# Block 1 of a two-block layer kernel: chunk decays inside the first chain, two output tiles among the attention, residual on VectorE, later gates

## The chip, the cores and the metric

The kernel runs on one core of a Trainium2 chip. The metric is device microseconds of one execution, as the median of several runs. The core has five engines that run beside each other and wait for one another on semaphores: TensorE (PE, matrix products into PSUM; its weight loads are listed apart as PEld), VectorE (DVE), ScalarE (ACT), GpSimd (POOL) and SyncE (SP), which only issues DMAs here. PSUM is the accumulator memory, SBUF the working memory.

## The reference, cut to what matters

512 tokens of width 1024 pass through two residual blocks, all in float32.

```python
# first_block
proj  = rms_norm(x, norm_pre_w) @ w_in            # 32 column tiles of 128, and 8 columns for beta and decay
beta  = sigmoid(d_b);  g = -exp(a_log) * softplus(d_a + dt_bias)
gc    = cumsum(g)                                  # per chunk: the "decays" exp(gc), exp(gc_last - gc)
o     = gated_delta_rule(silu(conv(d_q)), silu(conv(d_k)), silu(conv(d_v)), g, beta)   # 4 heads ("gdn")
mixed = concat([moba_attention(a_q, a_k, a_v) * silu(a_z), rms_norm(o) * silu(d_z)]) @ w_out
x     = x + rms_norm(mixed, norm_post_w)           # the residual
# second_block, token mixers: 8 channel groups i of 7 projections each
p  = rms_norm(x, norm1_g) @ w_in                   # 56 tiles: xa, ga, vb, bb, cb, ma, mb for every i
ya = rg_lru(conv(xa), gates r and i from two 128x128 matrices) * gelu(ga)
yb = bb * conv(cb * vb);  x = x + (sigmoid(ma)*ya + sigmoid(mb)*yb) @ w_out
# then a PEER layer: top-16 of product keys, 16384 experts, and a last norm
```

## The kernel before, in words

Activations lie transposed, channels on the 128 partitions and 512 tokens along the free axis. Every projection is kept near float32 by a split: an operand becomes a high part `hi` (in the format fp32r, by ScalarE, L194 or L258) and a low part `lo` (the difference, on VectorE or GpSimd, L195 or L259), and `mm3` adds three products, hi·hi, lo·hi and hi·lo. One output tile of 128 channels by 512 tokens is thus 8 slices of the contraction times 3, which makes 24 matmuls (L219). `wblock` loads one 128-column block of a weight matrix (512 KB), casts the high part on ScalarE and subtracts on GpSimd unless told otherwise; three such blocks fit (`WB = 3`). The tag `mm` of the pool `pmm` has two PSUM banks, the tags `pg` and `pt` two each, and `pu` of the pool `ps2` two.

The order of PE's instructions in blocks 1 and 2 is the program's own (`manual_schedule`). The order on the other engines comes from a planner at build time, which puts the instructions in a list by its own estimates; each engine then works through its list in order, and an instruction that waits holds up what stands behind it.

Block 1 begins with the norm statistics while the tiles 0 and 1 of the projection run slice by slice (L640), and computes beta and the decay logarithms `gl_` from 8 extra columns (L643 to L656). The generator `filler` yields after every matmul of the remaining 30 projection tiles; `pump(n)` takes n of them. `pump(54)` comes first. Then two small matmuls sum `gl_` into `gc` (L660, L661) and four small instructions make `gc`, `ngc`, `egc`, `egl`. After that a loop runs up to two gated-delta chains (`gdn(h)`) and one attention chain (`attn(j)`) at a time; after each step of a chain it pumps some filler (6 matmuls divided by the chains that run). The last steps of `gdn` normalize a head (`on`, L531), let three loop turns pass, and transpose it into `mixed` (L535). `attn` ends with `oa` (L591), a transpose (L595) and a copy into `mixed` (L596).

When all chains are done, the eight slices of `mixed` are multiplied with the silu gates `zg` (L695) and split into the `xhi` and `xlo` buffers, which the projection's operands held until then. The output projection follows, eight tiles of 24 matmuls (L704), with squares (L274) for the second norm. Its factor `rb2` is a power on GpSimd (L292), transposes (L295) and a ScalarE copy (L296). 16 small matmuls (`warm`, L183) run behind it. The residual (L721, L722) multiplies `mo` by `rb2` and adds the input `xk`; five slices are on VectorE, the slices 2, 5 and 7 (`XPOOL`) on GpSimd. As slices come out they are split (L258, L259), squared for block 2's first norm, and multiplied into block 2's first three tiles at once (L738), which `g.ahead` holds.

Block 2 loops over the channel groups i. For i = 0 the three tiles xa, ga, vb come from `g.ahead`; xa is scaled (L798), convolved (L809, L811) and split to `xch` and `xcl`; then come the gate products `pr` and `pi` (L822), and behind them in PE's order the tiles bb, cb, ma and mb, and for i = 1 again xa.

## Time and profile before

| | us |
|---|---|
| median of 3 runs (2138.79 to 2141.41) | 2138.96 |
| the profiled execution | 2143.05 |
| its span on the chip | 2141.3 |
| TensorE busy in the span | 2059.9 |
| VectorE busy | 1553.5 |
| GpSimd busy | 1000.3 |
| ScalarE busy | 845.9 |

All stretches are given in microseconds from the start of the span. Block 1 takes the first 423 or so, the residual and the start of block 2 reach to about 500, block 2 runs to roughly 750, and the PEER layer takes the rest. A row of the timeline that ends in x8 stands for eight instructions, and its second number is the stretch they cover. The number in brackets is the time for which the engine sat idle before, and who released it. The granted clock of TensorE is a share of full speed: 1.00 is 2.4 GHz, 0.50 is 1.2 GHz. A matmul of 512 columns counts as busy for its whole passage, so PE can be fully busy at half the clock.

### The profile page before, as it was taken

Reading aid. Unit: us, or ns where it says so; the run is one execution under the profiler, and the core shown is the slowest. Engines: PE = TensorE matmul, PEld = TensorE weight load, DVE = VectorE, ACT = ScalarE, POOL = GpSimd, SP = SyncE. Lnnn points to the kernel's source line nnn. Section 1 sums busy time; section 2 is a strip of 40 time slices with the busy share of each in tenths; the row PEclk is TensorE's granted clock in tenths of the full one; section 3 lists DMA queues with packets and bytes.
Section 4 is the critical chain, followed back from the end, with each engine's and each line's share of the span. In section 5 each row is a group of like instructions: output and inputs, shape, how many; then the busy total and the mean of one; then the engine's idle time right before and its main releaser. Section 6 shows DMA issues by size and latency. Waiting matters only on the chain.

```text
span 2141.3 us, 28911 instructions
## 1 busy us (share of the span) xinstructions
PE 2059.9 (96%) x10584; PEld 1783.5 (83%) x10584; DVE 1553.5 (73%) x2663; ACT 845.9 (40%) x1340; POOL 1000.3 (47%) x834
## 2 busy tenths in 40 slices
PE   8999999979999999887999999999999999999998
PEld 5787887758887878776999999999999999999886
DVE  5535446276777776999996897878787888887674
ACT  4434434344444444233454333333333333333333
POOL 3544252445566554775784254444444444444220
PEclk8999999979999999999999999999999999999999
DMA  4101121212322323222458999889889888898573
GB/s 154 54 30 50 55 70 54 79 60 89 98 89 89 99 89 109 83 76 69 183 230 302 319 353 313 301 301 310 297 307 309 293 311 302 300 313 271 192 257 101
DMA packets 147149, 394.07 MB, mean 184 GB/s; under 512 B 11584, under 2 KB 60864, under 8 KB 145216
## 3 DMA queue, kind: packets, MB, share of 16 engines
q1 hardware_dynamic: 110144, 258.00, 35.6%
q0 software_dynamic: 36864, 134.23, 18.1%
q8 instruction: 83, 1.36, 0.3%
q14 instruction: 58, 0.48, 0.1%
HBM read 364.92 MB, written 27.26 MB: 183 GB/s over the span
## 4 chain that ended last, share of the span: by engine, by line
PE 51%; DVE 8%; POOL 1%; DMA 1%; issue 1%; ACT 0%; POOLq 0%; DVEq 0%; SPq 0%; ACTq 0%
PE acc L1181 24%; PE ups L219 22%; PE gp L1074 4%; DVE t L1035 1%; DVE idxf L1006 1%; POOL pr L1002 1%; DVE ind L1037 1%; DVE ind L1034 1%; DVE eq L998 1%; DVE val L1036 1%; DMA gate<-gd 1%; DVE val L1033 1%; DVE cand L977 0%; DVE wlo L195 0%; DVE pos L1037 0%
## 5 line engine op out<-in xcount | busy, mean ns | idle before, releaser
L194 ACT CAST whi<-wraw 128x1024 fp32r<-128x1024 f32 x248 | 260.1, 1049 | 420.4 <-PE ups L219 290.8
L195 POOL TENSOR_TENSOR wlo<-wraw,whi 128x1024 fp32r<-128x1024 f32 x127 | 312.7, 2468 | 225.4 <-ACT whi L194 222.6
L1102 POOL DMA_INDIRECT row<-u,idx x128 | 199.1, 1556 | 267.8 <-DVE row L1108 228.3
L1102 POOL DMA_INDIRECT row<-v,idx x128 | 182.4, 1425 | 279.3 <-DVE xtok L1120 267.8
L219 PE MATMUL mm<-xhi,whi 128*128 128x512 f32 x856 | 234.7, 406 | 5.2 <-ACT xhi L194 3.6
L1181 PE MATMUL acc<-vhi,cl 128*128 128x512 f32 x768 | 237.6, 390 | 0.0
L1181 PE MATMUL acc<-vlo,ch 128*128 128x512 f32 x768 | 237.1, 389 | 0.4 <-DVE vlo L195 0.4
L1181 PE MATMUL acc<-vhi,ch 128*128 128x512 f32 x768 | 237.0, 389 | 0.0
L219 PE MATMUL mm<-xhi,wlo 128*128 128x512 f32 x856 | 233.2, 403 | 0.0
L219 PE MATMUL mm<-xlo,whi 128*128 128x512 f32 x856 | 226.9, 397 | 0.0
L219 PE MATMUL ups<-xhi,whi 128*128 128x384 f32 x1024 | 206.4, 339 | 7.9 <-DVE best L1033 6.6
L219 PE MATMUL ups<-xlo,whi 128*128 128x384 f32 x1024 | 202.9, 337 | 0.0
L219 PE MATMUL ups<-xhi,wlo 128*128 128x384 f32 x1024 | 201.9, 336 | 0.0
L219 PEld LDWEIGHTS ups<-xhi,whi 128*128 128x128 f32 x1024 | 182.1, 189 | 17.8 <-issue 8.7
L219 PEld LDWEIGHTS mm<-xhi,whi 128*128 128x128 f32 x856 | 157.6, 192 | 40.6 <-issue 8.0
L219 PEld LDWEIGHTS mm<-xhi,wlo 128*128 128x128 f32 x856 | 159.4, 191 | 36.8 <-issue 5.1
L219 PEld LDWEIGHTS mm<-xlo,whi 128*128 128x128 f32 x856 | 156.9, 189 | 34.3 <-issue 4.9
L195 DVE TENSOR_TENSOR wlo<-wraw,whi 128x1024 fp32r<-128x1024 f32 x121 | 149.1, 1232 | 49.7 <-ACT whi L194 49.7
L219 PEld LDWEIGHTS ups<-xlo,whi 128*128 128x128 f32 x1024 | 180.0, 189 | 0.1
L219 PEld LDWEIGHTS ups<-xhi,wlo 128*128 128x128 f32 x1024 | 179.8, 188 | 0.0
L194 ACT CAST ch<-act 128x384 fp32r<-128x384 f32 x128 | 65.7, 513 | 269.6 <-PE acc L1181 269.2
L1181 PEld LDWEIGHTS acc<-vlo,ch 128*128 128x128 f32 x768 | 144.1, 188 | 30.9 <-DVE vlo L195 0.8
(462 smaller groups left out, 3535.4 us busy)
## 6 DMA issues: line engine op xcount, KB each, us to landing
wraw<-uT SPq DMA_DIRECT2D x128, 512.0 KB
vring<-v SPq DMA_DIRECT2D x128, 512.0 KB
wraw<-w SPq DMA_DIRECT2D x88, 512.0 KB
gd<-stage SPq DMA_DIRECT2D x12, 2048.0 KB
gate<-gd SPq DMA_DIRECT2D x32, 768.0 KB
wraw<-wo SPq DMA_DIRECT2D x16, 512.0 KB
wraw<-wq SPq DMA_DIRECT2D x16, 512.0 KB
xr<-xT SPq DMA_DIRECT2D x8, 256.0 KB
```

The source lines that it names most:

```text
L194: nc.scalar.copy(hi, src)
L195: return (lo_eng or nc.vector).tensor_tensor(out=lo, in0=src, in1=hi.bitcast(F32), op=OP.subtract)
L219: nc.tensor.matmul(out, w(k), x(k), start=j == 0, stop=j == len(ps) - 1)
L998: V.tensor_tensor(out=eq[:, :n], in0=rank[:, :n], in1=pf[:, q].rearrange("p t k -> p (t k)")[:, None, :].to_broadcast([128, n, 16]), op=OP ...
L1002: nc.gpsimd.tensor_tensor(out=pr[:, :n].rearrange("p c (t k) -> p c t k", t=4), in0=eq[:, :n].rearrange("p c (t k) -> p c t k", t=4), in1= ...
L1006: V.tensor_reduce(out=g.idxf[:, :, h * 16 + 4 * q:h * 16 + 4 * q + 4], in_=pr[:, :n].rearrange("p c (t k) -> p t k c", t=4), axis=AX.X, op ...
L1033: V.max(out=v[:, 0:8], in_=x)
L1034: V.max_index(out=i[:, 0:8], in_max=v[:, 0:8], in_values=x)
L1035: V.match_replace(out=y[:, :n], in_to_replace=v[:, 0:8], in_values=x, imm_value=-3.0e38)
L1074: nc.tensor.matmul(ps[:, j * 128:(j + 1) * 128], oh[:, 1, j, :], oh[:, 0, j, :], start=True, stop=True)
L1102: nc.gpsimd.indirect_dma_start(out=r, out_offset=None, in_=g.a[tab], in_offset=bass.IndirectOffsetOnAxis(ap=s.idx[:, i:i + 1], axis=0))
L1181: nc.tensor.matmul(acc[m][e], l[:, ts], r[:, e * 512:(e + 1) * 512], start=False, stop=end and l is cl)
```

## The change

- The low part of the weight block of tile 1 is subtracted by VectorE, no longer by GpSimd.
- The two `gcp` matmuls and the five instructions behind them move into the first chain, behind two more of its turns (`decays`), and no longer stand ahead of the loop.
- `filler` goes on after the projection: for each slice k of `mixed`, once it is there, it does the gate product and the split (`merge`) and the slice's three products for the output tiles 0 and 1 (`first_out`). Slice 3, the last head pair of the attention, follows after the loop. The tiles 2 to 7 run as before.
- The transposes that end a `gdn` chain come six turns after its normalization, not three.
- All eight slices of the residual are on VectorE, in order. The warm-up matmuls there are 8, not 16. Squares are added in pairs (`add_pair`) and sent to the statistics in five sets of four products, not two. The last products are cut so that the power on GpSimd lies beside six of them.
- In block 2, i = 0, the tiles bb and cb are multiplied ahead of the gate products, into the two banks of `pu`.

```diff
@@ -137,10 +137,9 @@
 
 WB = 3
 WARM = 16
-WARM2 = 16
+WARM2 = 8
 PRE = 54
 VLO = (3, 4)
-XPOOL = (2, 5, 7)
 
 
 class K:
...
@@ -273,6 +273,18 @@
             self.sq = self.pool.tile([128, T], F32, name="ssq", tag="cth")
         self.g.nc.scalar.activation(self.sq, src, AF.Square)
 
+    def add_pair(self):
+
+        k, self.n = self.n, self.n + 1
+        if k < KD - 2 and k % 2 == 0:
+            self.acc = self.sq
+            return
+        if k < KD - 2:
+            self.g.nc.vector.tensor_tensor(out=self.sq, in0=self.acc, in1=self.sq, op=OP.add)
+        for tt in range(4):
+            self.g.nc.tensor.matmul(self.st[:, tt:tt + 1], self.sq[:, tt * 128:(tt + 1) * 128], self.g.ones,
+                                    start=k == 1 and tt == 0, stop=k == KD - 1 and tt == 3)
+
     def add(self):
 
         k, self.n = self.n, self.n + 1
@@ -285,11 +297,19 @@
 
     def finish(self, rb, rtok, tag="pg", dim=1024, eps=1e-6):
 
+        self.root(rtok, dim, eps)
+        self.spread(rb, rtok, tag)
+
+    def root(self, rtok, dim=1024, eps=1e-6):
         g = self.g
         nc = g.nc
         ms = self.pool.tile([128, 4], F32, name="ms")
         nc.vector.tensor_scalar(out=ms, in0=self.st[:, :4], scalar1=1.0 / dim, scalar2=eps, op0=OP.mult, op1=OP.add)
         nc.gpsimd.tensor_tensor(out=rtok, in0=ms, in1=g.nhalf[:, :4], op=OP.pow)
+
+    def spread(self, rb, rtok, tag="pg"):
+        g = self.g
+        nc = g.nc
         bc = g.pg.tile([128, 512], F32, name="bc", tag=tag)
         for tt in range(4):
             nc.tensor.transpose(bc[:, tt * 128:(tt + 1) * 128], rtok[:, tt:tt + 1].to_broadcast([128, 128]), g.ident)
@@ -399,6 +419,28 @@
             for i, k in enumerate((4, 5, 6, 7, 0, 1, 2, 3)):
                 yield from gate_in(24 + i, k)
 
+            o1["hi"], o1["lo"], o1["rb"], o1["rtok"] = operands(g)
+            o1["w"] = [wblock(g, g.a["wo1"][k]) for k in range(2)]
+            o1["ps"] = [g.pmm.tile([128, 512], F32, name="mm", tag="mm") for k in range(2)]
+            for k in (4, 5, 6, 7, 0, 1, 2):
+                while ("m", k) not in done:
+                    yield "blocked"
+                merge(k)
+                yield from first_out(k)
+
+        o1 = {}
+
+        def merge(k):
+            V.tensor_tensor(out=mixed[:, k, :], in0=mixed[:, k, :], in1=zg[:, k, :], op=OP.mult)
+            split(g, o1["hi"][:, k, :], o1["lo"][:, k, :], mixed[:, k, :])
+
+        def first_out(k):
+
+            for (h_, l_), ps in zip(o1["w"], o1["ps"]):
+                for j, (w, x) in enumerate(((h_, o1["hi"]), (l_, o1["hi"]), (h_, o1["lo"]))):
+                    nc.tensor.matmul(ps, w[:, k, :], x[:, k, :], start=k == 4 and j == 0, stop=k == 3 and j == 2)
+                    yield
+
 
         def gdn(h):
             dk, dq, dv = [res.pop((n, h)) for n in ("dk", "dq", "dv")]
@@ -421,9 +463,14 @@
             fq = R.tile([128, 4], F32, name="fq")
             V.tensor_tensor(out=fv, in0=rk, in1=beta[:, :, h], op=OP.mult)
             V.tensor_tensor(out=fa, in0=fv, in1=rk, op=OP.mult)
-            V.tensor_tensor(out=fk, in0=fa, in1=egc[:, :, h], op=OP.mult)
             V.tensor_scalar(out=fq, in0=rq, scalar1=128.0 ** -0.5, scalar2=None, op0=OP.mult)
             yield
+            if h == 0:
+
+                yield
+                yield
+                decays()
+            V.tensor_tensor(out=fk, in0=fa, in1=egc[:, :, h], op=OP.mult)
 
             gb = four(lambda o, b: nc.tensor.transpose(o, gc[:, b, h:h + 1].to_broadcast([128, 128]), g.ident))
             E = t4("E", "cth")
@@ -529,11 +576,11 @@
             V.tensor_tensor(out=ro, in0=ro, in1=fq, op=OP.mult)
             on = t4("on", bufs=2)
             V.tensor_tensor(out=on, in0=po, in1=ro[:, :, None].to_broadcast([128, 4, 128]), op=OP.mult)
-            yield
-            yield
-            yield
+            for _ in range(6):
+                yield
             ps = four(lambda o, b: nc.tensor.transpose(o, on[:, b, :], g.ident))
             nc.scalar.activation(mixed[:, 4 + h, :].rearrange("p (b t) -> p b t", b=4), ps, AF.Copy, scale=vec(g, "gnw", 0))
+            done.add(("m", 4 + h))
 
 
         def attn(j):
@@ -594,6 +641,7 @@
             yield
             ps = four(lambda o, b: nc.tensor.transpose(o, oa[:, b, :], g.ident), "pt")
             nc.scalar.copy(mixed[:, j, :].rearrange("p (b t) -> p b t", b=4), ps)
+            done.add(("m", j))
 
         warm(g, WARM)
         gate = P.tile([128, 8], F32, name="gate")
@@ -623,7 +671,7 @@
 
         with tc.manual_schedule(engines={mybir.EngineType.PE}):
 
-            w0 = [wblock(g, None, raw=g.w0[i], lo_eng=(V, nc.gpsimd)[i]) for i in range(2)]
+            w0 = [wblock(g, None, raw=g.w0[i], lo_eng=V) for i in range(2)]
             p0 = [g.pmm.tile([128, 512], F32, name="mm", tag="mm") for i in range(2)]
             st = RmsSum(g, R)
             pba = g.pg.tile([128, 512], F32, name="bap", tag="pt")
@@ -655,19 +703,22 @@
             softplus(g, P, fl(gl_), fl(z), 16)
             V.tensor_tensor(out=gl_, in0=gl_, in1=nea[:, None, :].to_broadcast([128, 4, 4]), op=OP.mult)
             pump(PRE)
-
-            ps = g.pg.tile([128, 512], F32, name="gcp", tag="pg")
-            nc.tensor.matmul(ps[:, :16], g.cst[:, C_U:C_U + 128], fl(gl_), start=True, stop=True)
-            nc.tensor.matmul(ps[:, 16:32], g.ones.to_broadcast([128, 128]), fl(gl_), start=True, stop=True)
             gc = P.tile([128, 4, 4], F32, name="gc")
             ngc = P.tile([128, 4, 4], F32, name="ngc")
             egc = P.tile([128, 4, 4], F32, name="egc")
             egl = P.tile([128, 4, 4], F32, name="egl")
-            V.tensor_copy(fl(gc), ps[:, :16])
-            V.tensor_scalar(out=fl(ngc), in0=ps[:, :16], scalar1=-1.0, scalar2=None, op0=OP.mult)
-            nc.scalar.activation(egc, gc, AF.Exp)
-            V.tensor_tensor(out=fl(egl), in0=ps[:, 16:32], in1=fl(gc), op=OP.subtract)
-            nc.scalar.activation(egl, egl, AF.Exp)
+
+            def decays():
+
+                ps = g.pg.tile([128, 512], F32, name="gcp", tag="pg")
+                nc.tensor.matmul(ps[:, :16], g.cst[:, C_U:C_U + 128], fl(gl_), start=True, stop=True)
+                nc.tensor.matmul(ps[:, 16:32], g.ones.to_broadcast([128, 128]), fl(gl_), start=True, stop=True)
+                V.tensor_copy(fl(gc), ps[:, :16])
+                V.tensor_scalar(out=fl(ngc), in0=ps[:, :16], scalar1=-1.0, scalar2=None, op0=OP.mult)
+                nc.scalar.activation(egc, gc, AF.Exp)
+                V.tensor_tensor(out=fl(egl), in0=ps[:, 16:32], in1=fl(gc), op=OP.subtract)
+                nc.scalar.activation(egl, egl, AF.Exp)
+
             mixed = g.xp.tile([128, 8, T], F32, name="mixed", tag="xr")
             zg = P.tile([128, 8, T], F32, name="zg")
             ready = {}
@@ -690,10 +741,10 @@
                     pump(-(-FILL // max(len(run), 1)))
                 if not run:
                     pump(FILL)
-            mhi, mlo, rb2, rt2 = operands(g)
-            for k in (4, 5, 6, 7, 0, 1, 2, 3):
-                V.tensor_tensor(out=mixed[:, k, :], in0=mixed[:, k, :], in1=zg[:, k, :], op=OP.mult)
-                split(g, mhi[:, k, :], mlo[:, k, :], mixed[:, k, :])
+            merge(3)
+            for _ in first_out(3):
+                pass
+            mhi, mlo, rb2, rt2 = o1["hi"], o1["lo"], o1["rb"], o1["rtok"]
 
             xk = [R.tile([128, T], F32, name=f"xk{k}", tag=("dk", "dq", "dv", "qT")[k % 4]) for k in range(KD)]
             for k in range(KD):
@@ -701,7 +752,7 @@
             mo = g.xp.tile([128, 8, T], F32, name="mo", tag="xr")
             st = RmsSum(g, R)
             for k in range(KD):
-                ps = proj_tile(g, wblock(g, g.a["wo1"][k]), mhi, mlo, (4, 5, 6, 7, 0, 1, 2, 3))
+                ps = o1["ps"][k] if k < 2 else proj_tile(g, wblock(g, g.a["wo1"][k]), mhi, mlo, (4, 5, 6, 7, 0, 1, 2, 3))
                 if k:
                     st.add()
                 st.square(ps)
@@ -717,26 +768,26 @@
             st = RmsSum(g, R)
 
             def residual(k):
-                e = nc.gpsimd if k in XPOOL else V
-                e.tensor_tensor(out=mo[:, k, :], in0=mo[:, k, :], in1=rb2, op=OP.mult)
-                e.tensor_tensor(out=mo[:, k, :], in0=mo[:, k, :], in1=xk[k], op=OP.add)
-
-            for k in XPOOL + (0, 1):
+                V.tensor_tensor(out=mo[:, k, :], in0=mo[:, k, :], in1=rb2, op=OP.mult)
+                V.tensor_tensor(out=mo[:, k, :], in0=mo[:, k, :], in1=xk[k], op=OP.add)
+
+            def products(k, tiles=(0, 1, 2)):
+                for t in tiles:
+                    (h_, l_), o = w[t], g.ahead[t]
+                    for j, (wt, x) in enumerate(((h_, g.b2[0]), (l_, g.b2[0]), (h_, g.b2[1]))):
+                        nc.tensor.matmul(o, wt[:, k, :], x[:, k, :], start=k == 0 and j == 0, stop=k == KD - 1 and j == 2)
+
+            for k in range(KD):
                 residual(k)
-            for k in range(KD + 1):
-                if k + 2 < KD and k + 2 not in XPOOL:
-                    residual(k + 2)
-                if k < KD:
-                    scaled_split(g, g.b2[0], g.b2[1], mo, "n1", [k])
-                    st.square(mo[:, k, :])
-                    st.add()
-                else:
-                    st.finish(g.b2[2], g.b2[3])
+                scaled_split(g, g.b2[0], g.b2[1], mo, "n1", [k])
+                st.square(mo[:, k, :])
                 if k:
-                    for o, (h_, l_) in zip(g.ahead, w):
-                        for j, (wt, x) in enumerate(((h_, g.b2[0]), (l_, g.b2[0]), (h_, g.b2[1]))):
-                            nc.tensor.matmul(o, wt[:, k - 1, :], x[:, k - 1, :], start=k == 1 and j == 0,
-                                             stop=k == KD and j == 2)
+                    products(k - 1)
+                st.add_pair()
+            st.root(g.b2[3])
+            products(KD - 1, (0, 1))
+            st.spread(g.b2[2], g.b2[3])
+            products(KD - 1, (2,))
         return mo
 
 
@@ -779,10 +830,10 @@
         ahead = g.ahead
         blk = [len(ahead)]
 
-        def emit_tile():
+        def emit_tile(ps=None):
             w = wblock(g, g.a["w2"][blk[0]], lo_eng=V if blk[0] in VLO else None)
             blk[0] += 1
-            return proj_tile(g, w, xhi, xlo)
+            return proj_tile(g, w, xhi, xlo, ps=ps)
 
         def next_tile():
             return ahead.pop(0) if ahead else emit_tile()
@@ -826,6 +877,9 @@
             ga = scaled("ga", ps=ps_ga)
             ps_vb = next_tile()
             vb = scaled("vb", ps=ps_vb)
+            if i == 0:
+
+                ahead += [emit_tile(g.ps2.tile([128, 512], F32, name="ah", tag="pu")) for _ in range(2)]
             gates(pr, 0)
             tr = t("tr")
             nc.scalar.activation(tr, pr, AF.Tanh, scale=0.5, bias=bh[:, i:i + 1])
```

## Rows read from the trace of the kernel before

**Rows 1.** The page: busy time and share of each engine; VectorE's weight subtractions.

```profile
PE 2059.9 (96%) x10584; PEld 1783.5 (83%) x10584; DVE 1553.5 (73%) x2663; ACT 845.9 (40%) x1340; POOL 1000.3 (47%) x834
...
L195 DVE TENSOR_TENSOR wlo<-wraw,whi 128x1024 fp32r<-128x1024 f32 x121 | 149.1, 1232 | 49.7 <-ACT whi L194 49.7
```

**Rows 2.** Windows of the span: busy time (instructions) by engine; PEclk is granted clock.

```profile
48.40:62.00 13.60, 13.60 (x62) 11.65 (x63) 2.62 (x12) 4.52 (x11) 6.68 (x4) 0.75 0.13 40
...
368.90:372.60 3.70, 3.63 (x31) 3.23 (x29) 3.22 (x6) 3.70 (x8) 0.00 (x0) 1.00 0.02 4
...
434.70:457.20 22.50, 19.47 (x79) 15.57 (x80) 15.01 (x21) 8.43 (x14) 4.74 (x8) 0.79 0.00 1
...
457.20:478.00 20.80, 11.40 (x40) 8.44 (x39) 16.93 (x14) 9.69 (x15) 9.39 (x7) 0.75 0.23 77
...
478.00:500.00 22.00, 22.00 (x99) 18.22 (x98) 11.95 (x12) 9.20 (x10) 13.46 (x8) 1.00 0.24 72
...
500.00:860.00 360.00, 357.23 (x1590) 292.20 (x1589) 262.07 (x323) 159.99 (x213) 213.01 (x140) 1.00 0.29 94
```

**Rows 3.** Waits of TensorE from 0 to 500 us: total, times, longest, in us.

```profile
PE pr L822 <- ACT xch L194: 6.3, 1, 6.3
...
PE mm L219 <- ACT xhi L194: 3.6, 1, 3.6
...
PE f L535 <- DVE on L531: 3.3, 2, 2.2
...
PE gcp L660 <- DVE gl__288 L656: 3.2, 1, 3.2
...
PE pr L822 <- DVE xcl L195: 3.1, 1, 3.1
```

**Rows 4.** Timeline of the start: begin, length, engine, instruction, idle before.

```profile
10.11 2.37 POOL L195 TENSOR_TENSOR wlo<-wraw,whi 128x1024 fp32r<-128x1024 f32 x1 [9.29 <-ACT whi L194]
...
10.69 2.33 DVE L259 SCALAR_TENSOR_TENSOR xlo<-xr,vec,xhi 128x512 fp32r<-128x512 f32 x1 [2.41 <-ACT xhi L258]
...
13.08 0.80 PE L640 MATMUL mm<-xlo,whi 128*128 128x512 f32 x1 [1.16 <-DVE xlo L259]
```

**Rows 5.** Timeline around the decay sums ahead of the loop.

```profile
48.38 0.58 PE L660 MATMUL gcp<-gl__288,cst 128*128 128x16 f32 x2 [3.19 <-DVE gl__288 L656]
...
48.66 0.63 ACT L409 ACTIVATE s<-dq 128x512 f32<-128x512 f32 x1
...
50.23 3.61 PE L219 MATMUL mm<-xhi,wlo 128*128 128x512 f32 x8
...
57.98 0.60 PE L428 MATMUL f<-cst,gc 128*128 128x128 f32 x4
```

**Rows 6.** Timeline behind the attention: where the second and the third output tile begin.

```profile
384.72 1.98 PE L219 MATMUL mm<-xhi,whi 128*128 128x512 f32 x8
...
390.16 1.98 PE L219 MATMUL mm<-xhi,whi 128*128 128x512 f32 x8
```

**Rows 7.** Timeline of the residual and of the start of block 2.

```profile
427.36 3.17 DVE L721 TENSOR_TENSOR mo<-mo,rb 128x512 f32<-128x512 f32 x2 [2.45 <-ACT rb L296]
...
434.74 0.79 PE L738 MATMUL mm<-xhi,whi 128*128 128x512 f32 x1 [2.90 <-ACT xhi L258]
...
446.28 0.74 DVE L259 SCALAR_TENSOR_TENSOR xlo<-mo,vec,xhi 128x512 fp32r<-128x512 f32 x1
...
446.95 0.68 DVE L280 TENSOR_TENSOR sacc<-sacc,ssq 128x512 f32<-128x512 f32 x1
...
454.26 0.95 PE L283 MATMUL st<-ones,ssq 128*128 128x1 f32 x8
...
457.84 0.59 ACT L296 COPY rb<-bc 128x512 f32<-128x512 f32 x1 [9.55 <-PE bc L295]
...
484.50 1.98 PE L219 MATMUL mm<-xhi,whi 128*128 128x512 f32 x8
...
501.11 0.69 DVE L878 SCALAR_TENSOR_TENSOR mlo<-ma,mhi 128x512 fp32r<-128x512 f32 x1 [0.70 <-ACT mhi L877]
```

More of the change, by code (lines that the diff above doesn't have):

```diff
@@ L225, in mm3, with proj_tile @@
         pass
-def proj_tile(g, w, xhi, xlo, ks=range(KD)):
-    ps = g.pmm.tile([128, 512], F32, name="mm", tag="mm")
+def proj_tile(g, w, xhi, xlo, ks=range(KD), ps=None):
+    if ps is None:
+        ps = g.pmm.tile([128, 512], F32, name="mm", tag="mm")
     hi, lo = w
```

## The prediction

> **What bounds the kernel now.** I read the page first: PE is busy for 2059.9 of 2141.3 us [rows 1], so the time can fall only where PE idles or runs at half clock, or where work is taken off it. Then the windows [rows 2]. From 500 to 860 us PE works 357.23 of 360.00 us at clock 1.00; nothing in that stretch is changed, and it should only move. Lost time stands before it. From 457.2 to 478 PE is busy for 11.40 of 20.80 us at clock 0.75, from 434.7 to 457.2 for 19.47 of 22.50 at 0.79. In the first row, 48.4 to 62, PE looks full (13.60 of 13.60) but had 0.75 of its clock: a quarter of 13.6 us, 3.4 us, went there with no idle time to show it. Third, the waits of PE [rows 3]: the gate product `pr` waits 6.3 us for `xch` and 3.1 for `xcl`, the first output tile 3.6 for the last slice of `mixed`, the transposes of `on` 3.3, the decay sums 3.2. Each of these five is touched by the change.
>
> The Trainium skill says the same of the first column (Perfetto Trace Analysis, Identifying the Most-Contended Engine): a matmul busy share is no measure of how near PE is to its best. By idle time alone the decays below would be worth 3.2 us and no more; the row with 0.75 says otherwise, so I count matmuls, not busy time.
>
> The unit is 0.227 us for a matmul of 512 columns at full clock: 24 take from 384.72 to 390.16 [rows 6]. At half clock it is about 0.43: eight were spread over 3.61 us [rows 5].
>
> **Part 1, the low part of tile 1 on VectorE.** GpSimd's subtraction took 2.37 us from 10.11, and VectorE's split beside it 2.33 us instead of the 0.74 of the same form [rows 4, 7]. PE waited for that split until 13.08. On VectorE alone the two take 1.23 (the mean of its other weight subtractions [rows 1]) and 0.74, from about 10.1: the split is there at 12.1, or at 11.5 if it goes first. Worth 1.0 us. Bounds 0 (VectorE is late again before `rb`) and 1.6.
>
> **Part 2, the decays.** Before, PE stood 3.19 us until 48.38 and then ran at half clock for some 7 us; the transposes of `gc` began at 57.98, with 18 filler matmuls behind `gcp` [rows 5]. After, with part 1's microsecond off everything: PE goes on at 44.2 with 12 matmuls (2.7 us) and reaches the l2 sums at 46.9. They need the square of `dq`, which ScalarE began at 48.66 and ended at 49.29 [rows 5], behind a tanh that waits for VectorE; so 48.3 here, a new stall of about 1 us, and the second half of the sums ends at 48.9. 18 matmuls (4.1 us), 53.0; the two sums, 0.6; the copy of `gc` and its handoffs, 0.4, in which PE has nothing; transposes at 54.0. That is 4.0 us earlier, with 30 fillers done and not 18 (12 × 0.227 = 2.7 us more): 6.7 us, less part 1's 1.0: 5.7. If VectorE has a long instruction in front of that copy, 1 to 2 us go; if the clock falls in the shorter stall too, 2 or 3; if ScalarE squares `dq` sooner, 1 comes. Bounds 2 and 7.
>
> **Part 3, the attention's end.** (a) The transposes of `on` waited 3.3 us [rows 3]. Counting pumps through the loop, the fourth head's had 18 fillers between normalization and transposes and will have 36, over 8 us; I take 3.0 off, bounds 1 and 3.3. (b) Tile 31 ended at 368.9 and the third output tile began at 390.16 [rows 6], 21.3 us later. In them are 48 output matmuls (10.9 us), 4.3 us of attention products (3.63 in the window from 368.9 [rows 2] and 0.65 of last transposes), and 6.1 us of waits and half clock. In the new order I count no turn in which `filler` is blocked, since slices 4 to 7 and 0 to 2 are done in time. But the split's buffers are those that tile 31 reads: its high parts can begin eight matmuls before tile 31 ends, its low parts only behind it. So one low part (0.68) is uncovered except for two matmuls: 0.5 us lost. At the end stands a bare chain: a copy of 0.59 [rows 7], a product of 0.68, a cast of 0.62 and handoffs, 2.1 us, then 0.3 for the last low part. The tiles 0 and 1 now hold both `mm` banks to the same end, so tile 2 waits for the first bank's square (0.60) and copy (0.68), less three matmuls: 0.7. Together 10.9 + 4.3 + 0.5 + 2.1 + 0.3 + 0.7 = 18.8, worth 2.5 us. Bounds −1.5 (the clock falls in these gaps as it did at 379, some 3 us, and ScalarE puts a cast of 1.05 in front) and 4.
>
> A rule of the Trainium skill speaks against this edit (Perfetto Trace Analysis, Matmuls): independent groups should rotate through the banks so that one's evacuation lies beside the next one's products. The rows of before have that rotation and no gap between tiles; by the rule alone the whole 1.3 us of evacuation would show, 0.6 more than I count.
>
> **Part 4, residual and block 2's first groups.** `rb2` comes at 427.33 as before. Then GpSimd's residual products lay beside VectorE's, and VectorE's first two took 3.17 us [rows 7], where one takes 0.68 alone; PE began at 434.74. After: GpSimd has only the weight split left that ends at 428.3. First product 1.6 us, sum 0.65, high part 0.72 on ScalarE: PE begins at 430.4. VectorE has 16 residual instructions, 8 splits and 3 sums of squares at a spacing of 0.63 (446.28 to 446.95 [rows 7]), 17 us, and is through at about 446. PE has, up to the last set of statistics, 63 matmuls (14.3 us) and five sets at 0.81 (454.26 to the next matmul at 455.07 [rows 7]), 4.05: 18.35 us, the longer. It waits 0.8 for the first low part, and I give it 4.3 us of half clock (2.15 lost): before, 0.79 over 22.5 us [rows 2] is 9.4 us at half clock, to about 444, and in the last 4.3 of them PE's matmuls came without a break. So the statistics end at 430.4 + 0.8 + 18.35 + 2.15 = 451.7, before at 455.07. The three added sets cost 2.4 us of PE in this; eight warm-ups fewer cost nothing by themselves, since PE waits there anyway. Then the power on GpSimd runs beside six matmuls; transposes, three more: block 2's next tile begins 2.7 us later, at 454.4. Its weights need the buffers of w2 tile 0, free two microseconds before. Tiles bb and cb, 48 matmuls: 465.3. `rb` is there at 454.4 (copy 457.84 to 458.43 before [rows 7]), and 12.1 us later, as before (458.43 to 470.5), `xcl`: 466.5, about when PE asks; VectorE is freer by GpSimd's absence. Gate products 1.4 us: 466.7. Before, the same work was done at 484.50 [rows 7]: 17.8 us. The 6.3 and 3.1 us waits are thus gone, and half clock with them.
>
> What is late next: VectorE. It has 16.93 + 11.95 = 28.9 us of work between 457.2 and 500 [rows 2], and PE, which now runs further ahead, wants the bank of xa, i = 1, at about 483, 28.5 us after `rb`. I take 1.5 us back: 16.3. Bounds 6 (see the first rival) and 19 (the clock never falls).
>
> **Sum.** 1.0 + 5.7 + 3.0 + 2.5 + 16.3 = 28.5 us. The profiled execution's 2143.05 becomes 2114.5. It lay 4.1 above the median, so the timed runs should give 2138.96 − 28.5 = 2110.5, rounded 2111.
>
> **Rivals.**
> First, VectorE's chain paces block 2's beginning. From `rb` (458.43) to the last split of i = 0 (501.11 and 0.69 [rows 7]) went 43.4 us; if that holds and xa of i = 1 stands behind it in VectorE's list, `xcl` of i = 1 comes at 504, and PE, there at 494, gives 10 us back. For it: 28.9 us of work in 28.5. Against it: in those 43.4 us VectorE waited for PE for a third of the time. Time: 2111 + 8.5 = about 2120; 0.2.
> Second, the clock falls in the gaps the change leaves (2.1 and 0.7 us at the attention's end, 1 us in the decays, 1 us ahead of the first product). For it: it fell behind the 3.19 and 3.6 us waits. Against it: behind the 2.2 us wait for `on` it stayed at 1.00. Price 3 + 2 + 2: about 2118; 0.12.
> Third, the clock holds through the residual and every bound falls well: 2.2 + 1.3 + 1.5 more, about 2105; 0.1.
> Fourth, the change does not do what it says: the planner puts the casts for bb and cb on ScalarE behind the convolution's instructions, so PE waits for weights instead of for `xch`. Then part 4 keeps only its 3.4 us up to the statistics: 12.2 less, part 1 to 3 stand: 2111 + 13 = 2124; 0.07. With parts 2 and 3 at their lower bounds too, 2135 to 2143, no change; 0.02.
> Fifth, slower: the lag of the first rival does not die out but recurs in each of the 7 later groups, because PE, two tiles ahead, meets two full banks every time. It decides from 28.5 / 7 = 4.1 us a group; at 5 us the time is 2111 + 35 = 2146. Against it: VectorE is busy for 262.07 of 360 us [rows 2]; 0.03.
>
> **How the numbers follow.** The forecast, 2107 to 2116, has 0.46. With the first to fourth rival, less their tails, 2102 to 2125 holds about 0.85. A difference under 0.2%, 4.3 us, can't be told from none. Faster by more: 0.95; within it: 0.02; slower: 0.03.
>
> **What would show it.** PE's wait for `gl_` gone and no half clock from 48 to 55; no wait over 0.5 us at L535; at the attention's end one gap near 2.1 us ahead of the last slice's matmul, and one near 0.7 ahead of tile 2; VectorE's residual instructions at 0.6 to 0.7 us; the first product of block 2 some 3 us behind `rb2`, the statistics' end 24.4 behind it; bb directly behind the ahead tiles; no wait of `pr` over 1 us. I am wrong if PE waits for VectorE over 3 us between 466 and 520 of the old count, or if 500 to 860 loses more than it did.

## The result, and the profile after

The changed kernel takes 2116.40 us (median of 4 runs, 2115.42 to 2118.02) beside 2140.18 for the kernel before on the same chip (2138.79 to 2141.77): ratio 0.9889, 95% interval 0.9872 to 0.9907. The forecast was 2111, with 2107 to 2116 as its middle range (0.46), which the median misses by 0.4 us, and 2102 to 2125 as its wide one (0.85), which holds it. The profiled execution took 2118.02 with a span of 2116.2, 1.6 above its median; that of before 2143.05 and 2141.3, 2.9 above the median of these four.

The page and the windows answer to [rows 1, 2]. TensorE's busy time fell by only 2.2 us while the span fell by 25.1: what went, in the profile's count, was idle time, 81.4 us before and 58.5 after.

```profile
PE 2057.7 (97%) x10600; PEld 1783.7 (84%) x10600; DVE 1541.0 (73%) x2667; ACT 846.4 (40%) x1340; POOL 987.1 (47%) x827
```

```profile
48.40:62.00 13.60, 13.33 (x71) 11.26 (x70) 4.71 (x15) 6.02 (x16) 9.07 (x8) 0.92 0.21 74
...
432.00:455.00 23.00, 20.50 (x95) 16.39 (x94) 13.59 (x14) 9.11 (x13) 13.76 (x13) 0.96 0.26 87
...
475.00:835.00 360.00, 354.53 (x1574) 288.88 (x1573) 261.63 (x322) 159.21 (x213) 212.81 (x140) 1.00 0.29 93
```

The last row is about the work that stood from 500 to 860 before, moved by 25 us: it loses 2.7 us more than it did (354.53 against 357.23), which the prediction had named as a sign of being wrong. The waits of TensorE up to 500 us answer to [rows 3]:

```profile
PE mm L778 <- ACT xhi L258: 2.4, 1, 2.4
PE mm L441 <- ACT xhi L193: 2.0, 1, 2.0
PE pr L873 <- DVE xcl L194: 1.7, 1, 1.7
PE mm L218 <- DVE bb L849: 1.6, 1, 1.6
...
PE mm L441 <- DVE xlo L194: 0.9, 1, 0.9
...
PE pr L873 <- ACT xch L193: 0.7, 1, 0.7
```

The waits for `gl_` and `on` are gone, those for `xch` and `xcl` are 2.4 us in place of 9.4, and that for the last slice of `mixed`, which now stands ahead of the last six products of the tiles 0 and 1, is 2.0 in place of 3.6. New are the bank that VectorE empties into `bb` (1.6) and the low part of the first slice of `mixed` in the filler (0.9).

Three timelines answer to [rows 4 to 6]: start, decays, end of the attention.

```profile
10.04 0.75 DVE L259 SCALAR_TENSOR_TENSOR xlo<-xr,vec,xhi 128x512 fp32r<-128x512 f32 x1
...
10.84 0.50 PE L688 MATMUL mm<-xlo,whi 128*128 128x512 f32 x1 [0.43 <-DVE xlo L259]
```

```profile
45.10 1.05 PE L359 MATMUL l2p<-ones,s 128*128 128x1 f32 x8 [0.41 <-ACT s L451]
...
47.75 3.31 PE L218 MATMUL mm<-xhi,whi 128*128 128x512 f32 x8
...
52.61 0.65 PE L475 MATMUL f<-cst,gc 128*128 128x128 f32 x4 [0.27 <-DVE gc L716]
```

```profile
354.49 0.40 PE L441 MATMUL mm<-xhi,whi 128*128 128x512 f32 x1
...
356.03 0.50 PE L441 MATMUL mm<-xlo,whi 128*128 128x512 f32 x1 [0.91 <-DVE xlo L194]
...
371.32 0.71 PE L441 MATMUL mm<-xhi,whi 128*128 128x512 f32 x1 [2.05 <-ACT xhi L193]
...
373.53 0.63 PE L441 MATMUL mm<-xlo,whi 128*128 128x512 f32 x1
374.14 2.43 PE L218 MATMUL mm<-xhi,whi 128*128 128x512 f32 x8
```

The next timeline holds the residual and block 2's first groups [rows 7]. In it look at what stands between `rb` (439.15) and the gates (450.77): on ScalarE two weight casts ahead of the copy of `rb`; on VectorE two weight subtractions ahead of `ca`, then an instruction of 1.5 us beside GpSimd; on ScalarE, when `xc` is ready, a tanh that waited for GpSimd and another cast ahead of `xch`; and a subtraction of 2.45 us beside GpSimd's 5.15.

```profile
411.81 2.10 DVE L771 TENSOR_TENSOR mo<-mo,rb 128x512 f32<-128x512 f32 x2 [2.45 <-ACT rb L316]
...
413.83 1.28 DVE L772 TENSOR_TENSOR mo<-mo,xk 128x512 f32<-128x512 f32 x2
...
415.32 0.50 PE L778 MATMUL mm<-xhi,whi 128*128 128x512 f32 x1 [2.44 <-ACT xhi L258]
...
437.25 2.00 ACT L193 CAST whi<-wraw 128x1024 fp32r<-128x1024 f32 x2 [6.14 <-PE mm L778]
...
438.32 2.36 DVE L194 TENSOR_TENSOR wlo<-wraw,whi 128x1024 fp32r<-128x1024 f32 x2 [1.77 <-ACT whi L193]
...
438.95 2.01 PE L218 MATMUL ah<-xhi,whi 128*128 128x512 f32 x8
439.15 0.58 ACT L316 COPY rb<-bc 128x512 f32<-128x512 f32 x1
...
444.52 2.93 DVE L862 SCALAR_TENSOR_TENSOR xc<-ca,vec,xc 128x512 f32<-128x512 f32 x2
...
448.63 0.63 ACT L908 ACTIVATE g<-g 128x512 f32<-128x512 f32 x1 [5.36 <-POOL ca L856]
449.17 1.04 ACT L193 CAST whi<-wraw 128x1024 fp32r<-128x1024 f32 x1
...
450.11 0.61 ACT L193 CAST xch<-xc 128x512 fp32r<-128x512 f32 x1
450.28 5.15 POOL L194 TENSOR_TENSOR wlo<-wraw,whi 128x1024 fp32r<-128x1024 f32 x2 [1.65 <-ACT whi L193]
...
450.75 2.45 DVE L194 TENSOR_TENSOR xcl<-xc,xch 128x512 fp32r<-128x512 f32 x1 [0.16 <-ACT xch L193]
450.77 0.50 PE L873 MATMUL pr<-xch,wah 128*128 128x512 f32 x1 [0.75 <-ACT xch L193]
...
453.25 0.72 PE L873 MATMUL pr<-xcl,wah 128*128 128x512 f32 x1 [1.75 <-DVE xcl L194]
...
455.05 2.80 PE L218 MATMUL mm<-xhi,whi 128*128 128x512 f32 x8
```

The beginning of each stage in both traces gives the gain by stage. The predicted column holds the terms of the sum (part 4 before its give-back):

| up to | before | after | gain so far | of the stage | predicted |
|---|---|---|---|---|---|
| tile 2 of the first projection | 32.65 | 28.41 | 4.2 | 4.2 | 1.0 |
| transposes of `gc`, 12 fillers more done (2.7 us) | 57.98 | 52.61 | 8.1 | 3.9 | 5.7 |
| end of tile 31 | 368.9 | 354.49 | 14.4 | 6.3 | 3.0 |
| third output tile | 390.16 | 374.14 | 16.0 | 1.6 | 2.5 |
| last statistics done | 455.07 | 436.22 | 18.9 | 2.8 | 3.4 |
| tile behind the first gates | 484.50 | 455.05 | 29.45 | 10.6 | 14.4 |
| gates of i = 1 | 511.70 | 483.1 | 28.6 | −0.9 | |
| gates of i = 2 | 551.2 | 524.7 | 26.5 | −2.1 | −1.5 |
| stage behind block 2 (third group of `scp`) | 848.43 | 823.53 | 24.9 | −1.6 | |
| end | 2141.3 | 2116.2 | 25.1 | 0.2 | |

### The profile page after: what moved, and what is told of

Read it like the earlier page. It is cut to its first block, busy times and chain, and to the rows that moved or that the text cites. A ratio compares the mean times of both kernels' runs of the same rounds, so it can differ in the third digit from the quotient of the medians.

```text
span 2116.2 us, 28926 instructions
## 1 busy us (share of the span) xinstructions
PE 2057.7 (97%) x10600; PEld 1783.7 (84%) x10600; DVE 1541.0 (73%) x2667; ACT 846.4 (40%) x1340; POOL 987.1 (47%) x827
## 4 chain that ended last, share of the span: by engine, by line
PE 68%; DVE 17%; POOL 4%; ACT 4%; issue 3%; DMA 1%; POOLq 0%; DVEq 0%; SPq 0%; ACTq 0%
PE acc L1235 24%; PE ups L218 21%; PE mm L218 9%; PE gp L1128 4%; PE f L359 3%; POOL wlo L194 2%; DVE t L896 1%; DVE xc L862 1%; DVE t L1089 1%; DVE ma L926 1%; DVE idxf L1060 1%; DVE yb L921 1%; DVE ind L1091 1%; DVE ind L1088 1%; POOL pr L1056 1%
## 5 line engine op out<-in xcount | busy, mean ns | idle before, releaser
L218 PE MATMUL mm<-xhi,whi 128*128 128x512 f32 x824 | 227.1, 408 | 3.7 <-DVE bb L849 3.7
L218 PE MATMUL mm<-xhi,wlo 128*128 128x512 f32 x824 | 223.1, 401 | 0.0
L218 PE MATMUL mm<-xlo,whi 128*128 128x512 f32 x824 | 219.9, 398 | 0.0
L218 PEld LDWEIGHTS mm<-xhi,whi 128*128 128x128 f32 x824 | 152.3, 194 | 42.1 <-issue 13.5
L218 PEld LDWEIGHTS mm<-xhi,wlo 128*128 128x128 f32 x824 | 152.2, 190 | 32.6 <-issue 3.3
L218 PEld LDWEIGHTS mm<-xlo,whi 128*128 128x128 f32 x824 | 151.3, 189 | 32.9 <-issue 4.9
```

The lines of the kernel that those rows point to most:

```text
L218: nc.tensor.matmul(out, w(k), x(k), start=j == 0, stop=j == len(ps) - 1)
```

## The experiments

"Before" is always the kernel before in the same lot on the same chip: 2139.93 with e1, e2, e3 and e5; 2140.46 with e4, e6, e7 and e8; 2141.81 with e9, e11, e12 and e13. A difference "from the change" is one of medians, from 2116.40. The medians of before differ by up to 1.9 us between lots (2139.93 to 2141.81), so a difference of two microseconds from the change is not shown by medians alone.

### The start

**e1: the kernel before with part 1 alone.**
```
-lo_eng=(V, nc.gpsimd)[i]
+lo_eng=V
```


> The kernel before with one edit alone: the low part of tile 1's weights on VectorE. Theory A (clock): with the split no longer late at 13.08 us PE has no gap behind its warm-up, the granted clock stays at 1.00 from 7 to 33 us (0.87 before), and tile 2 of the projection begins near 28.5 us, as in the changed kernel, not at 32.65: 4.1 us. Rival B (wait only, as predicted): the gain is the late split's 1.0 us, tile 2 near 31.6, the clock as before. The time by A: 4 us under the kernel before; by B 1 us.

Measured: 2139.61, ratio 0.9997 (0.9982 to 1.0012): nothing that this interval, some 4 us faster to 2.5 slower, can tell. Yet its trace is 4.5 us ahead at the transposes of `gc` (53.47), and tile 2 begins at 28.53. In the trace it loses this between 113 and 125; but that execution (2144.43) lay 4.8 us above its median, so this shows how one execution lost it and not why the medians agree. The windows of this kernel and of the one before, over the same stretch:

```profile
105.00:130.00 25.00, 22.43 (x113) 17.93 (x111) 10.74 (x19) 8.69 (x19) 10.19 (x8) 0.80 0.07 22
```

```profile
105.00:130.00 25.00, 22.43 (x149) 18.68 (x147) 11.97 (x23) 10.06 (x23) 10.54 (x9) 1.00 0.07 23
```

The busy time is the same to the last digit, 22.43 us; the one did 113 matmuls in it, the other 149. Both traces have one wait for `dec` of nearly the same length there:

```profile
113.76 1.16 PE L339 MATMUL f<-dk 128*128 128x128 f32 x8 [2.57 <-ACT dec L433]
...
115.37 1.80 PE L339 MATMUL f<-p,D 128*128 128x64 f32 x8
```

```profile
118.27 1.16 PE L339 MATMUL f<-dk 128*128 128x128 f32 x8 [2.58 <-ACT dec L433]
...
119.73 1.00 PE L339 MATMUL f<-p,D 128*128 128x64 f32 x8
```

Behind the one wait the clock fell for some 10 us, behind the other it did not. Two more traces have this wait of 2.6 us: in e13 the clock fell for some 10 us, in e2 for 3.4.

**e12: the change with the low part of tile 1 on GpSimd again.**
```
-lo_eng=V
+lo_eng=(V, nc.gpsimd)[i]
```


> The changed kernel with the low part of tile 1 on GpSimd again. Alone on the kernel before, this edit began everything 4.5 us earlier at 53 us and left nothing of it in the time. Theory A: there the gain fell to waits with fallen clock between 62 and 337 us, which the changed kernel no longer has; so undoing it here costs 3 to 5 us, and the granted clock from 7 to 20 us falls to about 0.75. Rival B: some later stage meets a time of its own (loads, GpSimd) and the start does not matter: under 1 us.

Measured: 2116.85, ratio 0.9885 (0.9858 to 0.9912), no difference that can be told; theory A failed, in its 3 to 5 us and in its clock. In the trace the wait for that split is 1.65 us (0.43 in the change), and tile 2 begins 1.1 us later. So part 1 is worth 1.1 to 1.2 at its place. The granted clock stays at 1.00 from 7 to 33 here, and in e13, which has the low part on GpSimd too. The half clock at the start of the trace of before (granted clock 0.74 from 7 to 20 us, about 3 us) thus belongs to that execution and not to the code: about 3 of the 4.2 us of the table's first stage are no gain of the change.

### Decays and attention

**e2: the change with the decays ahead of the loop again.**
```
-            if h == 0:
-                yield
-                yield
-                decays()
+        decays()
```


> The changed kernel with the decay sums ahead of the loop again, no extra turns in the first chain. Theory A (parts add up): PE stands some 3 us for the decay logarithms, runs at half clock behind it, and everything from 62 us on is about 4.0 us later than in the changed kernel; the stretch 62 to 337 keeps its own gain. Rival B (alignment): the 12 matmuls by which the first chain moved are also what removed the other waits of the stretch 62 to 337 (TensorE idle 8.1 us before, 3.1 after); then PE idles there for over 6 us again and the loss is 7 us or more.

Measured: 2122.32, ratio 0.9905 (0.9877 to 0.9933): 5.9 us behind the change. Its gap of 3.2 us ahead of the decay sums is back. In the traces it is 2.4 us behind at the transposes of `gc` (0.36 ahead, with 12 fillers fewer done) and 7.0 behind at the first output product, so about 4.6 come in between; its waits from 60 to 340 us show that the later chains lie differently (0.8 for `X` and none for `dec` in the change; idle time there 6.24 against 3.14, and half clock took 3.4 us against 1.7):

```profile
PE f L359 <- ACT dec L475: 2.6, 1, 2.6
PE f L531 <- DVE X L528: 2.5, 4, 1.0
```

Part 2 reaches beyond its place. The reading is that 12 fillers done earlier put every later chain at another distance from its fillers; the waits fit it, but no run isolates it.

**e3: the change with three turns in place of six.**
```
-for _ in range(6):
+for _ in range(3):
```


> The changed kernel with three turns, not six, between a head's normalization and its transposes. Theory A: only the waits of these transposes come back: 1 to 3.3 us in one or two waits at that line, and the time rises by 1 to 3 us. Rival B: the whole surplus of the stretch 62 to 337 us and the attention's end (6.3 us against the 3.0 predicted) hangs on these turns: the end of tile 31 comes 5 us or more later than in the changed kernel. Rival C: the waits came from VectorE's list being held up by GpSimd at that place, and do not return: under 0.5 us.

Measured: 2129.89, ratio 0.9938 (0.9915 to 0.996): 13.5 us behind, the dearest undoing of all. Its first output product comes 13.3 us later (367.77), as rival B had it. Idle time from 60 to 340 us is 6.86 (3.14 in the change), and the granted clock costs another 6.8 there (1.7). Behind 340 the wait for `on` is back with 2.25 us. Two of its waits before that are absent or shorter in the change:

```profile
PE po L558 <- DVE vn L555: 1.8, 1, 1.8
PE f L581 <- ACT vb L513: 1.4, 1, 1.4
```

Much of the 13.5 is the clock. Five of the six executions took 2128.77 to 2131.41 at a mean granted clock of 0.986 to 0.988; the sixth had 0.991 and took 2121.76, 5.4 behind the change, whose clock was 0.989 to 0.990.

**e13: the kernel before with six turns alone.**
```
-yield
-yield
-yield
+for _ in range(6):
+    yield
```


> The kernel before with six turns, not three, ahead of a head's last transposes, and nothing else. Theory A (waits only): the 3.3 us of waits at that line go, and no more: 2136 to 2138 us. Rival B (what the undoing showed, 13.5 us): the turns also move the later chains off their waits and the clock holds: 5 us or more, under 2135. Rival C: in the old order other waits take their place: within 1 us.

Measured: 2138.81, ratio 0.9982 (0.997 to 0.9994): 3.0 us, with an interval from 1.3 to 6.4. That is the size of part 3a, but loosely: the before of this lot is the slowest, those of the other lots lie only 1.1 to 1.7 us above 2138.81, and theory A's 2136 to 2138 is missed. In the trace both waits for `on` are gone, a wait of 1.5 us for `vn` is new, the 2.6 us for `dec` stays, and behind it the clock fell from 117 to 127, at a wait where in the trace of before it did not. So the same edit is worth some 3 us alone, and 13.5, or 5.4 where the clock held, on top of the rest.

**e8: the change with fillers between the two l2 sums.**
```
+        if h == 0 and qi == 0:
+            yield
...
-                yield
```


> The changed kernel with six filler matmuls between the two l2 sums of the first head, and so one turn fewer behind them (the decays stay behind the same number of fillers). Theory A: the half clock from 47.7 to 50.9 us comes from the stretch of one-column products at 43.6 to 46.0 with its 0.4 us wait for the square of dq; with six matmuls between, the wait goes, the clock stays at 1.00 over 45 to 51, and the transposes of gc begin 1.5 to 2 us earlier. Rival B: the clock falls there in any case, and only the 0.4 us are won.

Measured: 2114.59, ratio 0.9882 (0.9865 to 0.9898); the intervals overlap. No half clock from 33 to 62, `gc` 0.5 us earlier, but a new wait of 1.4 us for `gc`. And of the runs whose decays and l2 sums are those of the change, e6, e7, e9 and e12 have the clock at 1.00 there as well, with `gc` as early (51.1 to 52.1), while in e3, e4 and e5 it fell. So the eight matmuls at half clock from 47.75 are no fixed cost, and the gap between the sums is not shown to be their cause.

**e4: the change with output tiles 0 and 1 behind the attention again.**
```
-            for k in (4, 5, 6, 7, 0, 1, 2):
-                ...
-                merge(k)
-                yield from first_out(k)
...
+            for k in (4, 5, 6, 7, 0, 1, 2, 3):
+                merge(k)
```


> The changed kernel with the two first output tiles behind the attention again (merges and all 48 matmuls after the loop). Theory A: the stretch from the end of tile 31 to the beginning of output tile 2 took 21.3 us before and 19.6 in the changed kernel; without the filler it is 20.5 to 22 again, and the time rises by 1 to 2.5 us. Rival B: the filler tiles cost PE a bank wait and a fallen clock of their own, as much as they hide: the time changes by under 0.5 us. Rival C: they hide more than that stretch shows (the attention's end had no filler and stalled earlier too): 4 us or more.

Measured: 2115.99, ratio 0.9883 (0.9867 to 0.99), the time of the change. The bare chain stands in one piece again, behind 3.5 us of waiting:

```profile
363.81 0.80 PE L218 MATMUL mm<-xhi,whi 128*128 128x512 f32 x1 [3.47 <-ACT xhi L193]
364.40 3.11 PE L218 MATMUL mm<-xhi,wlo 128*128 128x512 f32 x8
```

From the end of tile 31 (353.2) to the third output tile (374.60) it takes 21.4 us, in the change 19.65. So the edit saves 1.75 at its place, as theory A had it, and the medians do not show it, as rival B had it.

### The residual

**e6: the change with three slices on GpSimd, issued first.**
```
-V.tensor_tensor(out=mo[:, k, :], ...)
+e = nc.gpsimd if k in (2, 5, 7) else V
+e.tensor_tensor(out=mo[:, k, :], ...)
...
+for k in (2, 5, 7):
+    residual(k)
```


> The changed kernel with slices 2, 5 and 7 of the residual on GpSimd again and issued first, all else kept (pairs, 8 warm-ups, cut products). Theory A (port): VectorE's products beside GpSimd's take 1.5 to 1.7 us again, not 0.65; the first matmul of block 2 comes 6 to 7.4 us behind rb2 (3.5 in the changed kernel, 7.4 before), the statistics end 3 to 4 us later, and the time rises by 3 us or more. Rival B: PE is the bound of this stretch anyway (63 matmuls and five sets), so later slices only eat its half-clock start: under 1.5 us.

Measured: 2123.11, ratio 0.9918 (0.9901 to 0.9934): 6.7 us behind. Fewer instructions on VectorE, and it is later. Its timeline shows each engine at 1.7 us an instruction while both work, and VectorE alone at 0.68:

```profile
412.21 3.41 DVE L773 TENSOR_TENSOR mo<-mo,xk 128x512 f32<-128x512 f32 x2
...
422.44 0.68 DVE L772 TENSOR_TENSOR mo<-mo,rb 128x512 f32<-128x512 f32 x1
```

```profile
410.03 3.38 POOL L772 TENSOR_TENSOR mo<-mo,rb 128x512 f32<-128x512 f32 x2
```

TensorE waits 4.98 us for the first product and 2.99 for the first low part; from the first statistics of the output projection (404.6) to the last of the residual (440.8) it takes 36.24 us against 28.96.

**e9: the change with 16 warm-up matmuls.**
```
-WARM2 = 8
+WARM2 = 16
```


> The changed kernel with 16 warm-up matmuls at the residual. PE idles from 413 to 415.3 us there and then runs at half clock to 419.2. Theory A: eight more fill that idle time, the clock stays at 1.00 or rises earlier, 1 to 2 us less. Rival B: they run past the first high part and push the products back: 0 to 1.5 us more. Rival C: both cancel: within 0.5 us.

Measured: 2111.17, ratio 0.9854 (0.983 to 0.9879): 5.2 us ahead of the change; how much of it is the edit's is open. The products begin at full clock, where those of the change ran at half until 419.2, and that stage takes 28.0 us (28.96 in the change, 29.1 in e12). But it takes 27.9 to 28.0 in e2, e4, e7 and e8 too, which have eight warm-ups, so even this microsecond is not shown to be the edit's. The rest is where the clock fell and where it did not: the four executions had a mean granted clock of 0.991 to 0.992, those of the change 0.989 to 0.990. Both e9 and e12 wait 1.74 us for `xcl`; the timeline of e9, then of e12:

```profile
450.40 0.51 PE L873 MATMUL pr<-xcl,wah 128*128 128x512 f32 x1 [1.74 <-DVE xcl L194]
450.74 0.40 PE L873 MATMUL pi<-xch,wah 128*128 128x512 f32 x1
```

```profile
451.48 0.59 PE L873 MATMUL pr<-xcl,wah 128*128 128x512 f32 x1 [1.74 <-DVE xcl L194]
451.87 0.63 PE L873 MATMUL pi<-xch,wah 128*128 128x512 f32 x1
```

Whether the longer warm-up keeps the clock up at the later wait, or chance did, these runs do not settle.

### Block 2's first gates

**e5: the change without two tiles ahead of the gates.**
```
-if i == 0:
-    ahead += [emit_tile(...) for _ in range(2)]
```


> The changed kernel without the two tiles ahead of the gate products. Theory A (as predicted in size): the waits for xch and xcl come back in full, 6 and 3 us, with half clock behind them, and PE begins the tile ma 12 to 14 us later; block 2 gives a part of that back since VectorE no longer lags, so the time rises by 9 to 12 us. Rival B (VectorE's list is the pace of the first group): VectorE's chain from rb to the gates of i = 1 is as long in both, and PE, early or late, meets it there: the time rises by under 5 us.

Measured: 2121.28, ratio 0.9904 (0.9877 to 0.9932): 4.9 us behind. The waits for `xch` and `xcl` (9.4 us before) are there again as one, half clock behind it:

```profile
448.23 0.80 PE L873 MATMUL pr<-xch,wah 128*128 128x512 f32 x1 [10.55 <-ACT xch L193]
```

Its gates of i = 1 come at 489.6, 6.5 us later than in the change; the stage behind block 2 begins at 826.25, only 2.7 later. Between these two points it takes 336.7 us, and the change 340.4: running ahead brings 6.5 us and gives 3.8 of them back. Counted from the last statistics, which come 1.4 us earlier here, the two tiles bring 8.0 and keep 4.2; the median has rival B's size.

**e7: the change with a third tile ahead (`ma`).**
```
+ahead.append(emit_tile())
```


> The changed kernel with a third tile, ma of i = 0, ahead of the gate products too. Theory A (xch and xcl are late by ScalarE's and VectorE's lists, 0.75 and 1.75 us behind the second tile): the third tile's 5.4 us cover both waits, the clock stays at 1.00 there, and gate products end 4 us earlier in PE's count; of that 2 to 4 us stay in the time. Rival B (VectorE paces the first two groups): the gates and with them VectorE's chain of i = 0 begin 3 us later, PE meets it at the first tiles of i = 1, and the time gains under 1 us or loses up to 3.

Measured: 2110.88, ratio 0.9862 (0.9846 to 0.9879): 5.5 us ahead of the change. The gates meet both operands, run at full clock and take the 1.4 us predicted (452.27 to 453.67); the wait for the bank of `bb` grows from 1.62 to 2.67:

```profile
452.27 0.40 PE L873 MATMUL pr<-xch,wah 128*128 128x512 f32 x1
...
452.74 0.40 PE L873 MATMUL pr<-xcl,wah 128*128 128x512 f32 x1
...
490.99 2.09 PE L218 MATMUL mm<-xhi,whi 128*128 128x512 f32 x8 [2.67 <-DVE bb L849]
```

Not all of the 5.5 is the tile's. Up to the last statistics the code is that of the change, yet the trace is 3.0 us ahead there (433.19 against 436.22). From there to the third group of `scp` it takes 383.1 us, 4.2 less than the change (387.3); e8 and e9, without the third tile and with the clock up at the gates, take 385.0 and 384.8. So the tile is worth 1.7 to 4.2 us at its place, and e9, without it, has the same median (2111.17).

**e11: e7 and e8 together, and eight warm-ups ahead of the last slice.**
```
+warm(g, 8)
 merge(3)
```


> The changed kernel with three edits: ma of i = 0 ahead of the gate products too, the l2 sums of the first head apart, and 8 warm-up matmuls in the gap ahead of the last slice's products. Theory A: the edits act in places of their own: 5.5 us (third tile, measured), 1.8 (l2 sums, measured) and 1.5 to 2 (the half clock from 371 to 376 goes): 2107 to 2108 us. Rival B: what they save is given back in block 2, where VectorE sets the pace of the first groups: 2110 to 2112, no better than the third tile alone.

Measured: 2110.08, ratio 0.9849 (0.9825 to 0.9873): no better than e7 alone. The half clock at 370 to 375 is gone; a dip at 176 to 179 stands in the trace of the change as well. Theory A had counted the 1.8 of e8 and the 5.5 of e7 as the edits' own, which neither run shows. e7, e9 and e11 are the best versions found, 5 to 6 us below the change, and their executions overlap (2109.43 to 2113.79).

## Why the prediction came out right, and where it was off

**The sum.** Up to the tile behind the first gates, 1.0 + 5.7 + 3.0 + 2.5 + 17.8 = 30.0 us were predicted and the traces differ by 29.45. That is better than its terms deserve, and in part luck: they are off in both directions, and about 3 of the 29.45 are the half clock at the start of the one trace of before, which no part of the prediction had. Behind it 4.35 us were given back, not 1.5: 2.85 short. Last, the median was reckoned by taking 28.5 off 2138.96, as if the whole difference of two traces were one of medians; the trace of before lay 4.1 above that median, that of the change only 1.6 above its own: another 2.5. Together 0.55 + 2.85 + 2.5 = 5.9, from 2110.5 to 2116.4. Of its two signs of being wrong, the later stretch losing more came true. The other, over 3 us of waiting for VectorE between 466 and 520 of the old count, is a close call: 1.75 for `xcl`, and 1.62 for the bank of `bb` just behind that stretch.

**Part 1 (1.0): right in size at its place** (1.1 to 1.2 in e12), but no median shows it.

**Part 2 (5.7): mechanism right.** 30 fillers stood before the transposes and the wait for `gl_` went, as predicted. The stall for the square was 0.41 and not 1 us; eight matmuls took 3.31 us at half clock behind it, 1.98 at full clock, which is most of what the stage lacks. A price for that, 2 or 3, was given. "No half clock from 48 to 55" failed in this trace; in four others of the same code there it holds.

**Part 3a (3.0): the step was too narrow.** Both waits at the transposes of `on` went, but so did the 2.6 for `dec` and 2.2 of 3.0 for `X`, against a new 1.0 for `vn` and 1.7 of half clock: 6.3 us in the stage. The prediction took the chains one by one; e2 shows that an edit at the first moves the waits of the later ones, which draw on the same fillers. That the edits do not add up is less sure: the undoings of e2 to e6 and e12 sum to 31.0 us where the change itself brought 23.8, but with the one execution of e3 in which the clock held they sum to 22.9.

**Part 3b (2.5): 1.6 in the trace, none that a median shows.** The bare chain cost 2.05 us (2.1 predicted), the low part 0.91 (0.5). But the clock fell behind that gap (0.63 a matmul from 371 on), as the second rival had it. For the bank, 0.7 was counted: the last matmul began at 373.53, tile 2 could have begun 0.43 later and began at 374.14, so 0.2 shows. The rule of the Trainium skill that spoke against the edit (Perfetto Trace Analysis, Matmuls: independent groups should rotate through the banks) would, by the prediction's estimate, have put 1.3 there. Half clock had left the evacuation more time, so this is no fair test of it; e4, which has the rotation, is no faster.

**Part 4, residual: right.** VectorE took 0.64 us an instruction, as predicted, once GpSimd's split had ended (two in 1.28 us from 413.83; two in 2.10 beside it). The first product came 3.5 us behind `rb2` (3.1 predicted), the last statistics 24.4 behind it (24.4). e6 shows the mechanism.

**Part 4, gates (17.8 in all): the term that was mis-sized.** Tiles `bb` and `cb` began 2.7 us behind the statistics and took 10.9, both as predicted. By the prediction's own terms the gates were to end at 467.4, not 466.7, since four of the six products come behind `xcl` (466.5). The gates then were to take 1.4 us and took 5.2 (449.87 to 455.05). The step that failed is "`rb` is there at 454.4 ..., and 12.1 us later ..., `xcl`: 466.5, about when PE asks; VectorE is freer by GpSimd's absence": `rb` came 0.8 later, behind two casts in ScalarE's list, and the 12.1 became 13.5 between casts, weight subtractions and GpSimd's work beside VectorE. Half clock from 453.4 on added some 0.9. It is the fourth rival turned round: there the weights were to stand behind the convolution and TensorE to wait for them, here their casts and subtractions stand ahead of it and TensorE waits for `xch` and `xcl`. (That rival's "12.2 less" is 12.9 by its own numbers, 16.3 − 3.4, and its time right.) With one tile more ahead the gates took the predicted 1.4 (e7).

**The give-back (1.5): first rival, in part.** VectorE does not hold up every group: the bank of `bb` costs 1.62 us once and 0.3 to 0.4 in each of the next six groups, where five such waits stood before as well. So the fifth rival is out. At the end of block 2 TensorE, now earlier, waits 0.70 for the load of `sk`.

## What to carry to other kernels

Before sizing a gain from a trace, look for half clock that only this execution has: compare two or three traces of the same code, and count as a gain only what they share. The same holds for a result: compare the granted clock of all executions before an edit is given the credit (e7, e9) or the blame (e3). Where work is moved ahead of a wait, follow the instructions that the wait hangs on through every engine's list, since a cast or a weight split that was harmless there is now in front. Fillers that cover several chains are one supply: test edits to them together and undo them one by one, since the same edit can look small alone (e13: some 3 us) and dear to undo (e3: 13.5 us, 5.4 where the clock held).

## What the runs showed of the hardware

- A wait costs its length, or its length and up to 5 us more, by whether the granted clock falls to half behind it. The same wait of 2.6 us left the clock at 1.00 in one trace (before), at half for 3.4 us in another (e2) and for some 10 us in two (e1, e13); 1.74 us ahead of the gates did either, in code that is the same there (e9, e12). None of the rows read here says beforehand which it will be.
- A busy share hides it wholly: 22.43 of 25.00 us with 113 matmuls at a mean clock of 0.80 (e1) or with 149 at 1.00 (before).
- VectorE and GpSimd, both on 128 x 512 f32 operands, took 1.7 us an instruction each; VectorE alone took 0.68. Three slices of eight handed over made the stage 7.3 us longer.
